# State-space loop prepared further ahead, swapped states from transposes, and the third block's tables loaded behind the last weights

## The chip, the cores and the metric

One core of a Trainium2 chip runs the whole program. TensorE (PE) does matmuls and transposes, VectorE (DVE) and ScalarE (ACT) the elementwise work, GpSimd (POOL) some of it, and SyncE (SP) issues the DMAs. The metric is the device time of one execution in microseconds (us), as the median of several; less is better.

## The reference

The program is a trunk of two layers over x (512 tokens, 1024 channels, fp32). The first mixes with attention, the second with a diagonal state-space model and a GLU; behind each stands an MLP with a squared ReLU.

```python
def reference(x, ...):
    for layer in range(DEPTH):
        h = rms_norm(x, mix_norm_g[layer])
        ...
            x = x + attn_mixer(h, ...)
        ...
            x = x + s5_mixer(h, ...)
        x = x + sq_relu_mlp(rms_norm(x, ffn_norm_g[layer]), w_ff1[layer], w_ff2[layer])

def s5_mixer(h, ...):
    ...
    def step(state, uc):
        bu = jnp.einsum('gpi,lbgi->lbgp', b_bar, uc.astype(jnp.complex64))
        _, hs = lax.associative_scan(combine, (a_el, bu), axis=0)
        hs = hs + a_pow[:, None] * state[None]
        y = jnp.einsum('gop,lbgp->lbgo', cmat, hs).real
        return hs[-1], y
    ...
    y = ys.transpose(2, 0, 1, 3, 4).reshape(B, S, D) + d_skip.astype(f32) * u
    g = jax.nn.gelu(y).astype(h.dtype)
    val, gate = jnp.split(g @ w_glu, 2, axis=-1)
    return val * jax.nn.sigmoid(gate)
```

There are 64 groups of 16 channels with 64 complex states each. A channel block below is 8 groups, that is 128 channels, so there are eight blocks.

## The kernel before

Every large product is made three times, from operands split into a high and a low fp32r part (`mm3`, L116 to L120). Weights come as 1 MB tiles `wraw` (DMA, L109), are cast to `whi` by ACT (L112), and DVE subtracts to get `wlo` (L113); the pool has two of each. The tile framework's scheduler sets the order of instructions on each engine, from the program's order and its own timeline. `behind(engine)` pins an instruction behind the newest one of an engine, `keep_in_program_order` fixes the row of DVE and POOL operations in the loop.

The stages are attention (to about 310 us), the first MLP (to 695.8), the state-space loop, the GLU's rest and the second MLP (from about 790 to the end). The first MLP has four groups of FF1 and FF2 products; an FF2 product has two column halves c = 0 and 1. Beside it a generator, `s5_tables` (L738 to L987), makes the loop's tables and puts them into DRAM; `pump` advances it by one step for each 6 us of planned matmul work. For each half block u its function `response` copies B into `bzh` and `bzl` (L946, L947) and at once multiplies with them on PE (L952 to L954). `B` itself is made by DVE (L888) and used by POOL products (L899 to L901).

Each block kb has four tables: tB, tT and tC of 1 MB and tR of 0.5 MB. `s5_open` (L1003) is called within the last FF2 product, behind the weights of c = 0, and loads the tables of kb 0 and 1 into a pool of two and those of kb 2 in pieces of 256 KB into the places of the MLP's input, `xhi` and `xlo`. The weights of c = 1 come behind that on SP. Later tables follow in the loop as places come free; tB and tC of kb 3 go into `wraw` tiles.

The loop in `s5` (L1121) runs ten iterations over eight blocks, with these steps:

- `s5_scale` (L1205): the block's input `ux` times the row norms on DVE, and the cast to Uh on ACT; `s5_split` (L1214): Ul on DVE.
- `s5_vee` (L1219): 24 matmuls U x tB, the copy `ys` on ACT (L1233), 8 transposes (L1237) that give V, real parts on partitions 0 to 63 and imaginary parts on 64 to 127.
- `s5_turn` (L1239): V times the rotation tR, one full product (L1246) and two of 64 partitions that read the other half of V (L1247, L1248); `s5_sub` (L1250) joins them.
- `s5_scan` (L1254): the scan over 64 chunks on DVE (L1260), behind the copy `dec` on ACT, then two products on POOL (L1261, L1262) that turn the states back; `s5_back2` (L1264) does the third on DVE, `s5_add` (L1269) joins them and casts Hh.
- `s5_out` (L1274): Hl on DVE, 48 matmuls U x tT and H x tC, two copies (L1293), 8 transposes (L1297); `s5_gelu` (L1299) makes the GLU's operands.

In iteration it the turn is that of block it, the scale, split and vee those of it + 1, the back2, add and out those of it - 1, the gelu that of it - 2. From it = 5 on `pieces` puts GLU products of the first output tile between; their weights are loaded and split at it = 4 (L1158).

Of the kernel before, what the change touches and what calls it, by code (L numbers as in the profile page):

```python
# [45 lines left out]
class Trunk:  # L46
# [690 lines left out]
    def s5_tables(self, s5p, s5b, s5c, s5d, gmix, side="right"):  # L737
# [6 lines left out]
        with ExitStack() as ctx:  # L744
# [196 lines left out]

            def response(u, wC):

                at = [bass.AP(tensor=t.tensor, offset=t.offset, ap=[t.ap[0], [64 + 16, 4], [1, 16]]) for t in bz]
                Bk = B[0][:, 4 * u:4 * u + 4]
                sc.copy(at[0], Bk)  # L946
                ve.tensor_sub(at[1], Bk, f32(at[0]))  # L947
                with tc.issue_after(self.last):
                    pk = self.ptp.tile([P, P], F32, name="pt")[:64]
                    for g4 in range(4):  # L950
                        wh, wl = (wC[:, a, g4, 16:144] for a in range(2))
                        pe.matmul(pk, bz[0][:, g4], wh, start=g4 == 0, stop=False)  # L952
# [21 lines left out]
            for u in range(16):  # L974
                now, made = made, make(u + 1) if u < 15 else None
                rotations(u // 2, u % 2)
                yield
                if wC is not None:
                    response(u - 1, wC)
                wC = split(u, *now)  # L980
                if u > 1:
                    expand(u - 2)
                yield
            response(15, wC)
            expand(14)
# [16 lines left out]

    def s5_open(self, places):  # L1003

        self.s5r, self.places, self.n_places = ExitStack(), places, 0
        self.tp = self.s5r.enter_context(self.tc.tile_pool(name="s5_t", bufs=2, side="right"))
        self.s5acc = self.tp.tile([P, S], F32, name="sacc", bufs=1)
        self.tabs = {}
        for kb in range(3):
            for n in ("tB", "tR", "tT", "tC"):  # L1010
                self.s5_load(kb, n, self.s5_pieces if kb == 2 else self.s5_whole)
        self.ux = []
# [68 lines left out]
    def s5(self, xT, w_glu, mlp, places):  # L1081
        nc, tc = self.nc, self.tc
        pe, ve, sc, gp = nc.tensor, nc.vector, nc.scalar, nc.gpsimd
        with ExitStack() as ctx:
            ctx.enter_context(places)
            sp = ctx.enter_context(tc.tile_pool(name="s5", bufs=2))
            sq = sp.tile([P, S], F32, name="gw")
            last = sc.activation(sq, xT[:, KT - 1], AF.Square).ins
# [9 lines left out]
            self.rsqrt(Rs, ps[:, :64], 1.0 / D, EPS, sp)  # L1098
            self.yv = sp.tile([P, 1024], F32, name="ys", bufs=1)
            dec = sp.tile([P, 8, 64], F32, name="dec", bufs=1)  # L1100
            gp.memset(dec[:, :, 0:1], 0.0)
            H = [[sp.tile([P, 8, 64], F32R, name=f"H{a}{b}", bufs=1) for a in "hl"] for b in range(2)]
            for a in range(2):
                for h in H[a]:
                    gp.tensor_scalar(h[:, :, 0:1], self.ones[:, 0:8][:, :, None], 0.0, None, op0=OP.mult)
            gT, st = [], {}
            pieces = {5: (0, 1), 6: (2, 3), 7: (4, 5), 8: (6,), 9: (7,)}
            half = [slice(0, 4), slice(4, 8)]
# [3 lines left out]
            for gs in half:  # L1112
                self.s5_split(0, st, gs)
                self.s5_vee(0, st, gs)

            def load(kb, n):
# [4 lines left out]
            for it in range(KT + 2):  # L1121
                if it < KT:
                    self.s5_turn(it, st, sp)
                if 0 < it <= KT:
                    self.s5_back2(it - 1, st)
                    if it != 3:
                        load(it + 2 if it < 3 else it + 1, "tR")
                if it + 1 < KT:
                    self.s5_scale(it + 1, st, Rs, sp, whole)
                if 0 < it <= KT:  # L1130
                    self.s5_add(it - 1, st, H[(it - 1) % 2])
                if it < KT:
                    self.s5_sub(it, st)
                if it + 1 < KT:
                    self.s5_split(it + 1, st, whole)
                    self.s5_vee(it + 1, st, whole)
                    if it == 0:
                        load(5, "tB")
                    elif 2 < it < 5:
                        load(it + 3, "tB")  # L1140
                    if 3 < it + 4 < KT:
                        with self.behind(nc.sync):
                            self.s5_load_x(it + 4)
                if it < KT:
                    self.s5_scan(it, st, dec)
                if 0 < it <= KT:
                    self.s5_out(it - 1, st, H[(it - 1) % 2], sp)
                    if it != 3:
                        load(it + 2 if it < 3 else it + 1, "tT")
                    if it < 3:  # L1150
                        load(it + 3, "tC")
                    elif it > 4:
                        load(it + 1, "tC")
                if it > 1:
                    gT.append([self.s5_place() for _ in "hl"])
                    self.s5_gelu(it - 2, st, gT[-1], sp)
                if it == 4:
                    W = self.glu_w(w_glu, 0)  # L1158
                    g = [self.glu(xT, W, gT, sp, 0, 0, [self.psp.tile([P, S], F32, name="s") for _ in range(2)])]
                for k in pieces.get(it, ()):  # L1160
                    g[0](k)
# [17 lines left out]
    def glu_w(self, w_glu, mp, eng=None):  # L1179

        return [self.load_wg([w_glu[kh * 512:(kh + 1) * 512, mp * 256:(mp + 1) * 256],
                              w_glu[kh * 512:(kh + 1) * 512, D + mp * 256:D + (mp + 1) * 256]], 4, eng)
                for kh in range(2)]

    def glu(self, xT, W, gT, sp, m, j, pss):
# [4 lines left out]
        def step(k):  # L1190
            if k is not None:
# [5 lines left out]
                return  # L1197
            th = sp.tile([P, S], F32, name="gw")
            sc.activation(th, pss[1], AF.Tanh, scale=0.5)
# [5 lines left out]
    def s5_scale(self, kb, st, Rs, sp, gs):  # L1205
        d = st.setdefault(kb, {})
        if "U" not in d:
            d["U"] = [sp.tile([P, 8, 64], F32R, name=f"U{a}", bufs=3) for a in "hl"]
        u = self.ux[kb][:, gs]
# [9 lines left out]
    def s5_vee(self, kb, st, gs):  # L1219
# [6 lines left out]
        for h in range(gs.start // 4, gs.stop // 4):  # L1226
            pc = self.mmp.tile([P, 4, P], F32, name="mm")
            for g4 in range(4):
# [3 lines left out]
                pe.matmul(pc[:64, g4], U[1][:, g8], tB(0, g8), start=False, stop=True)  # L1232
            sc.copy(vc[:, 4 * h:4 * h + 4], pc[:64])  # L1233
        if d["V"] is None:
            d["V"] = self.mmp.tile([P, 8, 64], F32, name="mm")
        for g8 in range(gs.start, gs.stop):
            pe.transpose(d["V"][:, g8], vc[:, g8], self.ident[64:, 64:])  # L1237

    def s5_turn(self, kb, st, sp):  # L1239
# [5 lines left out]
        R, V = d["R"], d["V"]  # L1245
        keep(ve.tensor_mul(d["t1"], V, R[0]))  # L1246
        keep(ve.tensor_mul(d["t2"][:64], V[64:], R[1][64:]))  # L1247
        keep(ve.tensor_mul(d["t2"][64:], V[:64], R[1][:64]))  # L1248

    def s5_sub(self, kb, st):  # L1250
        d = st[kb]
        self.tc.keep_in_program_order(self.nc.vector.tensor_sub(d["t1"], d["t1"], d["t2"]))

# [20 lines left out]
    def s5_out(self, kb, st, H, sp):  # L1274
# [5 lines left out]
        tT, tC = self.tabs[kb, "tT"], self.tabs[kb, "tC"]  # L1280
        ys = self.yv[:64].rearrange("p (l g o) -> p l g o", l=8, g=8)
        for h in range(2):
# [16 lines left out]
    def s5_gelu(self, kb, st, g, sp):  # L1299

        ve, sc = self.nc.vector, self.nc.scalar
        yT = st.pop(kb)["y"].rearrange("p l c -> p (l c)")
        w = sp.tile([P, S], F32, name="gw")
        sc.activation(w, yT, AF.Gelu_apprx_tanh)
# [4 lines left out]
class Mlp:  # L1309
# [41 lines left out]
    def run(self, emit=None, during=None, every=0.0, before_last=None, keep=False, halves=False):  # L1351
# [7 lines left out]
        with self.ctx if not keep else ExitStack(), tc.tile_pool(name="ffn_a", bufs=1) as pool:  # L1359
# [10 lines left out]
            for g in range(groups):  # L1370
# [30 lines left out]
                for c in range(2):  # L1401
                    W = [T.load_w(self.w2[g * GF * P + kh * 512:g * GF * P + (kh + 1) * 512,
                                          c * 512:(c + 1) * 512]) for kh in range(2)]
                    if last and c == 0 and before_last is not None:
                        with T.behind(nc.sync):
                            before_last()
                    for d4 in range(4):
# [29 lines left out]
def trunk(nc, tc, i, out):  # L1437
    with ExitStack() as ctx:
# [11 lines left out]
                              lambda xT: Mlp(T, xT, gf[0], i["w_ff1"][0], i["w_ff2"][0], "left"))  # L1450
        mlp.run(emit=lambda d, s: T.s5_emit(xT, d), before_last=lambda pool=mlp.pool: T.s5_open(pool), keep=True,
                during=T.s5_tables(i["s5p"], i["s5b"], i["s5c"], i["s5d"], i["mix_norm_g"][1]), every=6.0)
# [50 lines left out]
```

## Time and profile before

| what | us |
|---|---|
| median of 3 runs (1234.62 to 1238.17) | 1237.62 |
| the profiled execution | 1243.23 |
| its span, from the first instruction to the last | 1241.5 |
| PE busy in it | 1162.7 (94%) |
| DVE, ACT, POOL busy | 790.9, 495.0, 260.8 |
| first to last turn of the loop | 708.6 to 790.8 |

The trace is of the profiled execution. A number in brackets behind a row is idle time of the engine just before it, with what ended it. The granted clock (PEclk) is a share of 2.4 GHz: 1.00 is that level, 0.50 the lower one of 1.2 GHz, and numbers between are a mix. The DMA share is the mean busy share of the core's 16 DMA engines; it can come out slightly above 1.

### The profile page before, as it was taken

What the parts mean: (1) busy time and instruction counts of PE and PEld (TensorE: products, weight loads), DVE (VectorE), ACT (ScalarE), POOL (GpSimd) and SP (SyncE); (2) the same over time, 40 slices, a digit from 0 to 9 for tenths busy, and PEclk for the clock granted to TensorE, in tenths of its full rate; (3) what the DMA queues carried; (4) which work ended last, traced back from release to release, by engine and by line L of the source; (5) the groups of instructions that cost most, each with busy time, mean ns of one, the idle gap of its engine ahead of it and who ended that gap; (6) DMA issues with size and microseconds to landing.
All of it is one profiled execution on the core that took longest, in us unless ns stands there. A gap on an engine that the chain in (4) does not pass through costs nothing. (4 is left out here: it accounts for less than half of the span.)

```text
span 1241.5 us, 16297 instructions
## 1 busy us (share of the span) xinstructions
PE 1162.7 (94%) x6232; PEld 965.8 (78%) x6232; DVE 790.9 (64%) x1389; ACT 495.0 (40%) x919; POOL 260.8 (21%) x261
## 2 busy tenths in 40 slices
PE   7999999999999888999997668999999999999998
PEld 6878987778888666878886557778888888888887
DVE  8887765758889987779553567534444354444444
ACT  5857774544513333342342145443332241331321
POOL 5461031214001987505100022201000000000000
PEclk9999997999999889999998778999999999999999
DMA  6301201115423467874788577514223322322421
GB/s 219 103 1 52 69 35 35 35 35 191 121 79 102 163 197 228 245 222 142 245 288 299 160 230 252 214 34 133 79 94 102 102 86 84 102 102 68 132 86 54
DMA packets 123758, 161.94 MB, mean 130 GB/s; under 512 B 15648, under 2 KB 72352, under 8 KB 120992
## 3 DMA queue, kind: packets, MB, share of 16 engines
q1 hardware_dynamic: 123680, 160.90, 40.0%
q8 instruction: 49, 0.80, 0.3%
q14 instruction: 29, 0.24, 0.1%
HBM read 133.75 MB, written 35.52 MB: 136 GB/s over the span
## 5 line engine op out<-in xcount | busy, mean ns | idle before, releaser
L113 DVE TENSOR_TENSOR wlo<-wraw,whi 128x1024 fp32r<-128x1024 f32 x132 | 172.5, 1336 | 84.0 <-ACT whi L112 83.3
L112 ACT CAST whi<-wraw 128x1024 fp32r<-128x1024 f32 x132 | 131.9, 1049 | 228.4 <-PE mm L119 124.1
L118 PE MATMUL mm<-ahi,whi 128*128 128x512 f32 (+1 forms) x352 | 135.9, 388 | 7.7 <-ACT whi L112 7.7
L118 PE MATMUL mm<-xhi,whi 128*128 128x512 f32 x344 | 137.0, 398 | 0.0
L119 PE MATMUL mm<-xlo,whi 128*128 128x512 f32 x344 | 135.8, 395 | 0.0
L119 PE MATMUL mm<-alo,whi 128*128 128x512 f32 (+1 forms) x352 | 135.4, 387 | 0.0
L120 PE MATMUL mm<-xhi,wlo 128*128 128x512 f32 x344 | 134.4, 396 | 0.0
L120 PE MATMUL mm<-ahi,wlo 128*128 128x512 f32 (+1 forms) x352 | 134.2, 386 | 0.1
L118 PEld LDWEIGHTS mm<-ahi,whi 128*128 128x128 f32 x352 | 66.5, 189 | 21.1 <-ACT whi L112 8.1
L120 PEld LDWEIGHTS mm<-xhi,wlo 128*128 128x128 f32 x344 | 64.9, 189 | 15.6 <-DVE wlo L113 0.8
L120 PEld LDWEIGHTS mm<-ahi,wlo 128*128 128x128 f32 x352 | 66.3, 188 | 13.6 <-DVE wlo L113 0.5
L119 PEld LDWEIGHTS mm<-alo,whi 128*128 128x128 f32 x352 | 66.6, 189 | 13.1
L118 PEld LDWEIGHTS mm<-xhi,whi 128*128 128x128 f32 x344 | 64.9, 189 | 15.1 <-issue 0.5
L119 PEld LDWEIGHTS mm<-xlo,whi 128*128 128x128 f32 x344 | 65.0, 189 | 14.5 <-issue 0.2
L1418 DVE TENSOR_TENSOR mm<-mm,bcast 128x512 f32<-128x512 f32 (+1 forms) x44 | 29.8, 684 | 70.1 <-PE mm L120 70.1
L118 PE MATMUL s<-xhi,whi 128*128 128x512 f32 x168 | 66.7, 397 | 0.4 <-DVE fp L1390 0.4
L120 PE MATMUL s<-ahi,wlo 128*128 128x512 f32 x168 | 66.1, 394 | 0.9 <-DVE wlo L113 0.8
L119 PE MATMUL s<-xlo,whi 128*128 128x512 f32 x168 | 66.5, 396 | 0.0
L120 PE MATMUL s<-xhi,wlo 128*128 128x512 f32 x168 | 66.3, 396 | 0.0
L118 PE MATMUL s<-ahi,whi 128*128 128x512 f32 x168 | 66.2, 395 | 0.0
L119 PE MATMUL s<-alo,whi 128*128 128x512 f32 x168 | 66.0, 393 | 0.0
L899 POOL TENSOR_TENSOR W<-PW,B 128x512 f32<-128x512 f32 x16 | 23.8, 1490 | 160.1 <-DVE B L888 141.4
(487 smaller groups left out, 2868.0 us busy)
## 6 DMA issues: line engine op xcount, KB each, us to landing
wraw<-in_w_ff SPq DMA_DIRECT2D x64, 1024.0 KB
dC<-wC SPq DMA_DIRECT2D x16, 512.0 KB
dB<-wB SPq DMA_DIRECT2D x16, 512.0 KB
wraw<-in_w_glu SPq DMA_DIRECT2D x16, 512.0 KB
tT<-dT SPq DMA_DIRECT2D x7, 1024.0 KB
wraw<-in_w_in SPq DMA_DIRECT2D x24, 256.0 KB
tB<-dB SPq DMA_DIRECT2D x6, 1024.0 KB
tC<-dC SPq DMA_DIRECT2D x6, 1024.0 KB
```

Of the source, the lines that this page charges most:

```text
L112: nc.scalar.copy(hi[:, s, :n], raw[:, s, :n])
L113: nc.vector.tensor_sub(lo[:, s, :n], raw[:, s, :n], f32(hi)[:, s, :n])
L118: te.matmul(ps, whi, xhi, start=start, stop=False)
L119: te.matmul(ps, whi, xlo, start=False, stop=False)
L120: self.last = te.matmul(ps, wlo, xhi, start=False, stop=stop).ins
L899: gp.tensor_mul(dst, pw[a][:, :, 1:9, None].to_broadcast(bc), B[a][:, gs][:, :, None, :].to_broadcast(bc))
L1418: ve.tensor_mul(ps[:, s], ps[:, s], self.Rb[:, s])
```

## The change

The change has three parts.

*Tables of kb 2.* `s5_open` takes c: for c = 0 it loads the tables of kb 0 and 1, for c = 1 those of kb 2, behind the weights of c = 1.

*The generator.* `place(u)` makes `bzh` and `bzl` in the step ahead of the one in which `response(u)` uses them; there is one step more at the end.

*The loop.* Block 1 is scaled ahead of the loop and block it + 2 in iteration it. Split and vee of it + 1 come right behind the turn. The scan goes to the end of the iteration. V is made twice, as it was and with its halves swapped, by 16 transposes; ACT copies the real part once more behind the imaginary one for that (the tile `ys` grows to 1536 columns). The turn is then two full products and `s5_sub` an addition. There are four Uh in place of three, one Hl in place of two, one `gw` in place of two. The raw GLU weights are requested at it = 4 and split at it = 5 and 6, and fewer GLU products stand at it = 5.

```diff
-            def response(u, wC):
+            def place(u):
...
                 sc.copy(at[0], Bk)
                 ve.tensor_sub(at[1], Bk, f32(at[0]))
+
+            def response(u, wC):
...
                 rotations(u // 2, u % 2)
+                if u:
+                    place(u - 1)
                 yield
...
+            place(15)
+            yield
             response(15, wC)
...
-    def s5_open(self, places):
-
+    def s5_open(self, places, c):
+
+        if c:
+            for n in ("tB", "tR", "tT", "tC"):
+                self.s5_load(2, n, self.s5_pieces)
+            return
...
-        for kb in range(3):
+        for kb in range(2):
             for n in ("tB", "tR", "tT", "tC"):
-                self.s5_load(kb, n, self.s5_pieces if kb == 2 else self.s5_whole)
+                self.s5_load(kb, n, self.s5_whole)
...
-            pieces = {5: (0, 1), 6: (2, 3), 7: (4, 5), 8: (6,), 9: (7,)}
+            pieces = {5: (0,), 6: (1, 2), 7: (3, 4), 8: (5, 6), 9: (7,)}
...
+            self.s5_scale(1, st, Rs, sp, whole)
...
                 if it < KT:
                     self.s5_turn(it, st, sp)
-                if 0 < it <= KT:
-                    self.s5_back2(it - 1, st)
-                    if it != 3:
-                        load(it + 2 if it < 3 else it + 1, "tR")
-                if it + 1 < KT:
-                    self.s5_scale(it + 1, st, Rs, sp, whole)
-                if 0 < it <= KT:
-                    self.s5_add(it - 1, st, H[(it - 1) % 2])
-                if it < KT:
-                    self.s5_sub(it, st)
                 if it + 1 < KT:
                     self.s5_split(it + 1, st, whole)
                     self.s5_vee(it + 1, st, whole)
...
+                if 0 < it <= KT:
+                    self.s5_back2(it - 1, st)
+                    if it != 3:
+                        load(it + 2 if it < 3 else it + 1, "tR")
+                    self.s5_add(it - 1, st, H[(it - 1) % 2])
                 if it < KT:
-                    self.s5_scan(it, st, dec)
+                    self.s5_sub(it, st)
+                if it + 2 < KT:
+                    self.s5_scale(it + 2, st, Rs, sp, whole)
...
+                if it < KT:
+                    self.s5_scan(it, st, dec)
                 if it == 4:
-                    W = self.glu_w(w_glu, 0)
+                    with self.behind(nc.sync):
+                        raw = [self.glu_raw(w_glu, 0, kh) for kh in range(2)]
+                if it in (5, 6):
+                    W = [] if it == 5 else W
+                    W.append(self.split_w(raw[it - 5], 4, 512))
...
-            sc.copy(vc[:, 4 * h:4 * h + 4], pc[:64])
+            sc.copy(vc[:, 4 * h:4 * h + 4, :P], pc[:64])
+        sc.copy(vc[:, gs, P:], f32(vc[:, gs, :64]))
         if d["V"] is None:
-            d["V"] = self.mmp.tile([P, 8, 64], F32, name="mm")
-        for g8 in range(gs.start, gs.stop):
-            pe.transpose(d["V"][:, g8], vc[:, g8], self.ident[64:, 64:])
+            d["V"] = [self.mmp.tile([P, 8, 64], F32, name="mm") for _ in range(2)]
+        for a in range(2):
+            for g8 in range(gs.start, gs.stop):
+                pe.transpose(d["V"][a][:, g8], vc[:, g8, 64 * a:64 * a + P], self.ident[64:, 64:])
...
-        keep(ve.tensor_mul(d["t1"], V, R[0]))
-        keep(ve.tensor_mul(d["t2"][:64], V[64:], R[1][64:]))
-        keep(ve.tensor_mul(d["t2"][64:], V[:64], R[1][:64]))
+        keep(ve.tensor_mul(d["t1"], V[0], R[0]))
+        keep(ve.tensor_mul(d["t2"], V[1], R[1]))
...
-                    if last and c == 0 and before_last is not None:
+                    if last and before_last is not None:
                         with T.behind(nc.sync):
-                            before_last()
+                            before_last(c)
```

The queue of SP within the last FF2 product, in the kernel before; `wraw` are the weights, `xlo` and `xhi` the pieces of kb 2:

```order
L1046 DMA tR_6850<-dR1_125 128x512 x2
L1051 DMA tT_6853<-dT1_117 128x2048
L1051 DMA tC_6855<-dC1_93 128x2048
L1051 DMA xlo_6871<-dT2_118 128x512
L1051 DMA xhi_6872<-dT2_118 128x512
L1051 DMA xlo_6877<-dC2_94 128x512
L1051 DMA xhi_6878<-dC2_94 128x512
L1051 DMA xlo_6879<-dC2_94 128x512
L1051 DMA xhi_6880<-dC2_94 128x512
L109 DMA wraw_7013<-in_w_ff2 128x4x512
L109 DMA wraw_7021<-in_w_ff2 128x4x512
```

The weights of c = 1 are the last two rows. The same queue after the change, from the first half of these weights on:

```order
L109 DMA wraw_6985<-in_w_ff2 128x4x512
L965 DMA dK7h_114<-Ks_6728 4x16x128
L965 DMA dK7l_115<-Ks_6728 4x16x128
L971 DMA dT7_123<-dK7h_114 128x4x128
L971 DMA dT7_123<-dK7l_115 128x4x128
L1062 DMA tB_6839<-dB0_84 128x2048
L1057 DMA tR_6841<-dR0_124 128x512 x2
L1062 DMA tT_6844<-dT0_116 128x2048
L1062 DMA tC_6846<-dC0_92 128x2048
L1062 DMA tB_6848<-dB1_85 128x2048
L1057 DMA tR_6850<-dR1_125 128x512 x2
L1062 DMA tT_6853<-dT1_117 128x2048
```

Then the table of kb 1 that is left, the second half of the weights, and only then kb 2:

```order
L1062 DMA tC_6855<-dC1_93 128x2048
L109 DMA wraw_6993<-in_w_ff2 128x4x512
L1062 DMA xlo_7001<-dB2_86 128x512
L1062 DMA xhi_7002<-dB2_86 128x512
L1062 DMA xlo_7003<-dB2_86 128x512
L1062 DMA xhi_7004<-dB2_86 128x512
```

So both halves of the weights now stand ahead of kb 2. Next, DVE in one iteration of the loop, it = 2, before (t1 and t2 are the turn's results, `ux_7057` the input of block 3):

```order
L1246 TENSOR_TENSOR t1_7437<-mm_7356,xlo_6865 128x512
L1247 TENSOR_TENSOR t2_7438<-mm_7356,xhi_6866 64x512
L1248 TENSOR_TENSOR t2_7438<-mm_7356,xhi_6866 64x512
L1267 TENSOR_TENSOR u2_7312<-t2_7311,tR_6850 64x512
L1211 TENSOR_TENSOR ux_7057<-ux_7057,Rs_7179 128x512
L1271 TENSOR_TENSOR t1_7310<-t1_7310,u2_7312 128x512
L1252 TENSOR_TENSOR t1_7437<-t1_7437,t2_7438 128x512
L1306 TENSOR_TENSOR xhi_7565<-gw_7566,xlo_7564 128x512
L1217 TENSOR_TENSOR Ul_7448<-ux_7057,Uh_7447 128x512
L1260 SCALAR_TENSOR_TENSOR t2_7438<-dec_7196,t1_7437 128x512
L1279 TENSOR_TENSOR Hl1_7201<-t1_7310,Hh1_7200 128x8x63
```

And after, in the same iteration (`ux_7326` is the input of block 4):

```order
L1266 TENSOR_TENSOR t1_7468<-mm_7367,xlo_7009 128x512
L1267 TENSOR_TENSOR t2_7469<-mm_7368,xhi_7010 128x512
L1235 TENSOR_TENSOR Ul_7393<-ux_7057,Uh_7392 128x512
L1286 TENSOR_TENSOR u2_7334<-t2_7333,tR_6850 64x512
L1290 TENSOR_TENSOR t1_7332<-t1_7332,u2_7334 128x512
L1271 TENSOR_TENSOR t1_7468<-t1_7468,t2_7469 128x512
L1229 TENSOR_TENSOR ux_7326<-ux_7326,Rs_7179 128x512
L1298 TENSOR_TENSOR H2_7200<-t1_7332,H1_7199 128x8x63
L1325 TENSOR_TENSOR xhi_7601<-gw_7602,xlo_7600 128x512
L1279 SCALAR_TENSOR_TENSOR t2_7469<-dec_7196,t1_7468 128x512
```

Ul moved to the place behind the turn, the scale is that of a later block, Hl moved ahead of the scan. Last, PE around the second half of V's transposes for block 2, before (H are the operands of `s5_out` for block 0):

```order
L1292 MATMUL pt_7398<-tC_6846,Hl0_7199 64x128
L1237 MATMUL mm_7356<-ident_73,ys_7195 128x64 x4
L1287 MATMUL pt_7398<-tT_6844,Uh_7206 64x128
L1288 MATMUL pt_7398<-tT_6844,Uh_7206 64x128
L1289 MATMUL pt_7398<-tT_6844,Ul_7207 64x128
```

And around the transposes of the swapped V after the change:

```order
L1311 MATMUL pt_7425<-tC_6846,H2_7200 64x128
L1306 MATMUL pt_7425<-tT_6844,Uh_7204 64x128
L1307 MATMUL pt_7425<-tT_6844,Uh_7204 64x128
L1308 MATMUL pt_7425<-tT_6844,Ul_7205 64x128
L1257 MATMUL mm_7368<-ident_73,ys_7195 128x64 x8
L1309 MATMUL pt_7425<-tC_6846,H0_7198 64x128
```

The swapped V is a row of eight transposes of its own that stands among the matmuls of `s5_out`, behind those that read Hl (`H2`).

## Rows read from the trace of the kernel before

**Rows 1.** Page, part 1: busy time, share, instructions of each engine.

```profile
PE 1162.7 (94%) x6232; PEld 965.8 (78%) x6232; DVE 790.9 (64%) x1389; ACT 495.0 (40%) x919; POOL 260.8 (21%) x261
```

**Rows 2.** Waits, 655 to 680 us: total, times, longest.

```profile
PE mm L118 <- ACT whi L112: 7.7, 1, 7.7
...
ACT whi L112 <- DMA wraw<-in_w_ff: 10.4, 2, 9.9
```

**Rows 3.** Timeline of SP and PE, 649 to 673 us: start, length, instruction.

```profile
649.93 0.32 SPq L1051 DMA_DIRECT2D tC<-dC  x1
...
659.30 0.32 SPq L1051 DMA_DIRECT2D xhi<-dC  x1
661.80 2.87 SPq L109 DMA_DIRECT2D wraw<-in_w_ff  x2
...
672.19 0.80 PE L118 MATMUL mm<-ahi,whi 128*128 128x512 f32 x1 [7.70 <-ACT whi L112]
```

**Rows 4.** Windows of the last FF2: length, engines busy (instructions), clock, DMA share, GB/s.

```profile
645.00:665.00 20.00, 19.49 (x86) 15.79 (x85) 9.71 (x15) 3.99 (x8) 0.00 (x0) 1.00 1.02 404
...
672.20:676.00 3.80, 3.80 (x10) 3.04 (x11) 3.80 (x4) 3.37 (x4) 0.00 (x0) 0.58 0.34 132
```

**Rows 5.** Waits of PE, 300 to 664 us.

```profile
PE pt L952 <- ACT bzh L946: 7.5, 2, 4.4
PE pt L954 <- DVE bzl L947: 6.3, 3, 4.1
```

**Rows 6.** Line L1246, the turn: instructions, durations in ns, first and last start.

```profile
L1246 DVE TENSOR_TENSOR t<-mm,tR x7: 691/692/693, 708.6 to 790.8; 128x512 f32<-128x512 f32 x7
```

**Rows 7.** Windows from turn to turn (PE, PEld, DVE, ACT, POOL busy; clock; DMA).

```profile
708.60:716.70 8.10, 4.45 (x32) 3.71 (x32) 5.20 (x8) 2.39 (x4) 2.55 (x2) 0.50 0.42 134
716.70:727.90 11.20, 7.08 (x64) 6.56 (x65) 6.90 (x11) 3.57 (x6) 2.86 (x3) 0.56 0.65 178
727.90:738.80 10.90, 8.16 (x86) 7.13 (x86) 7.46 (x12) 6.46 (x10) 2.84 (x2) 0.84 0.80 273
738.80:754.40 15.60, 11.59 (x107) 9.86 (x108) 10.90 (x13) 8.09 (x14) 3.19 (x2) 0.78 0.89 297
754.40:768.40 14.00, 10.99 (x82) 8.91 (x83) 9.74 (x13) 5.28 (x9) 2.85 (x2) 0.76 0.75 242
768.40:779.70 11.30, 9.91 (x117) 8.31 (x117) 7.48 (x11) 5.70 (x11) 2.86 (x2) 1.00 0.67 238
779.70:790.80 11.10, 8.33 (x71) 6.99 (x72) 7.51 (x12) 4.52 (x8) 2.87 (x2) 0.85 0.63 238
```

**Rows 8.** Waits, 720 to 800 us.

```profile
DVE t L1246 <- PE mm L1237: 18.5, 5, 4.2
```

**Rows 9.** Chain that ended last, 768 to 782 us: start, length, what.

```profile
769.53 0.06 PE pt L1287
...
771.22 8.36 DMA tR<-dR
```

**Rows 10.** Timeline of one period, DVE, POOL and PE.

```profile
727.87 0.69 DVE L1246 TENSOR_TENSOR t<-mm,xlo 128x512 f32<-128x512 f32 x1 [4.25 <-PE mm L1237]
...
733.61 1.22 DVE L1260 TENSOR_TENSOR_SCAN t<-dec,t 128x512 f32<-128x512 f32 x1
...
734.97 1.57 POOL L1261 TENSOR_TENSOR u<-t,xhi 64x512 f32<-64x512 f32 x1 [8.86 <-DVE t L1260]
736.62 1.27 POOL L1262 TENSOR_TENSOR t<-t,xlo 128x512 f32<-128x512 f32 x1
...
737.40 0.46 PE L1237 MATMUL mm<-ident,ys 64*128 64x64 f32 x4
```

**Rows 11.** Window 400 to 420 us, columns as in rows 4.

```profile
400.00:420.00 20.00, 16.08 (x75) 12.65 (x73) 20.00 (x16) 9.06 (x15) 19.92 (x16) 0.98 0.34 118
```

**Rows 12.** Timeline of PE: eight transposes of V in two periods.

```profile
715.29 1.36 PE L1237 MATMUL mm<-ident,ys 64*128 64x64 f32 x8
...
767.66 0.71 PE L1237 MATMUL mm<-ident,ys 64*128 64x64 f32 x8
```

More of the change, by code (lines that the diff above doesn't have):

```diff
@@ L1086, in s5 @@
             sp = ctx.enter_context(tc.tile_pool(name="s5", bufs=2))
-            sq = sp.tile([P, S], F32, name="gw")
+            sq = sp.tile([P, S], F32, name="gw", bufs=1)
             last = sc.activation(sq, xT[:, KT - 1], AF.Square).ins
@@ L1098, in s5 @@
             self.rsqrt(Rs, ps[:, :64], 1.0 / D, EPS, sp)
-            self.yv = sp.tile([P, 1024], F32, name="ys", bufs=1)
+            self.yv = sp.tile([P, 1536], F32, name="ys", bufs=1)
             dec = sp.tile([P, 8, 64], F32, name="dec", bufs=1)
             gp.memset(dec[:, :, 0:1], 0.0)
[L1102 to L1105, printed above, removed]
+            H = [sp.tile([P, 8, 64], F32R, name=f"H{a}", bufs=1) for a in range(3)]
+            for h in H:
+                gp.tensor_scalar(h[:, :, 0:1], self.ones[:, 0:8][:, :, None], 0.0, None, op0=OP.mult)
+            H = [(H[a], H[2]) for a in range(2)]
             gT, st = [], {}
-            pieces = {5: (0, 1), 6: (2, 3), 7: (4, 5), 8: (6,), 9: (7,)}
+            pieces = {5: (0,), 6: (1, 2), 7: (3, 4), 8: (5, 6), 9: (7,)}
             half = [slice(0, 4), slice(4, 8)]
@@ L1140, in s5 @@
                         load(it + 3, "tB")
-                    if 3 < it + 4 < KT:
-                        with self.behind(nc.sync):
-                            self.s5_load_x(it + 4)
-                if it < KT:
-                    self.s5_scan(it, st, dec)
+                if 0 < it <= KT:
[3 more added lines that the diff above has]
+                    self.s5_add(it - 1, st, H[(it - 1) % 2])
+                if it < KT:
+                    self.s5_sub(it, st)
+                if it + 2 < KT:
+                    self.s5_scale(it + 2, st, Rs, sp, whole)
+                if 3 < it + 4 < KT:
+                    with self.behind(nc.sync):
+                        self.s5_load_x(it + 4)
                 if 0 < it <= KT:
@@ L1156, in s5 @@
                     self.s5_gelu(it - 2, st, gT[-1], sp)
+                if it < KT:
+                    self.s5_scan(it, st, dec)
                 if it == 4:
-                    W = self.glu_w(w_glu, 0)
+                    with self.behind(nc.sync):
+                        raw = [self.glu_raw(w_glu, 0, kh) for kh in range(2)]
+                if it in (5, 6):
+                    W = [] if it == 5 else W
+                    W.append(self.split_w(raw[it - 5], 4, 512))
+                if it == 5:
                     g = [self.glu(xT, W, gT, sp, 0, 0, [self.psp.tile([P, S], F32, name="s") for _ in range(2)])]
@@ L1179, in glu_w, with glu_raw @@
     def glu_w(self, w_glu, mp, eng=None):
-        return [self.load_wg([w_glu[kh * 512:(kh + 1) * 512, mp * 256:(mp + 1) * 256],
-                              w_glu[kh * 512:(kh + 1) * 512, D + mp * 256:D + (mp + 1) * 256]], 4, eng)
-                for kh in range(2)]
+        return [self.split_w(self.glu_raw(w_glu, mp, kh), 4, 512, eng) for kh in range(2)]
+    def glu_raw(self, w_glu, mp, kh):
+        return self.raw_w([w_glu[kh * 512:(kh + 1) * 512, mp * 256:(mp + 1) * 256],
+                           w_glu[kh * 512:(kh + 1) * 512, D + mp * 256:D + (mp + 1) * 256]], 4)
     def glu(self, xT, W, gT, sp, m, j, pss):
@@ L1197, in step @@
                 return
-            th = sp.tile([P, S], F32, name="gw")
+            th = sp.tile([P, S], F32, name="gw", bufs=1)
             sc.activation(th, pss[1], AF.Tanh, scale=0.5)
@@ L1207, in s5_scale @@
         if "U" not in d:
-            d["U"] = [sp.tile([P, 8, 64], F32R, name=f"U{a}", bufs=3) for a in "hl"]
+            d["U"] = [sp.tile([P, 8, 64], F32R, name="Uh", bufs=4), sp.tile([P, 8, 64], F32R, name="Ul", bufs=3)]
         u = self.ux[kb][:, gs]
@@ L1245, in s5_turn @@
         R, V = d["R"], d["V"]
[L1246 to L1248 removed]
+        keep(ve.tensor_mul(d["t1"], V[0], R[0]))
+        keep(ve.tensor_mul(d["t2"], V[1], R[1]))
     def s5_sub(self, kb, st):
         d = st[kb]
[L1252 removed]
+        self.tc.keep_in_program_order(self.nc.vector.tensor_add(d["t1"], d["t1"], d["t2"]))
     def s5_scan(self, kb, st, dec):
@@ L1280, in s5_out @@
         tT, tC = self.tabs[kb, "tT"], self.tabs[kb, "tC"]
-        ys = self.yv[:64].rearrange("p (l g o) -> p l g o", l=8, g=8)
+        ys = self.yv[:64, :1024].rearrange("p (l g o) -> p l g o", l=8, g=8)
         for h in range(2):
@@ L1302, in s5_gelu @@
         yT = st.pop(kb)["y"].rearrange("p l c -> p (l c)")
-        w = sp.tile([P, S], F32, name="gw")
+        w = sp.tile([P, S], F32, name="gw", bufs=1)
         sc.activation(w, yT, AF.Gelu_apprx_tanh)
@@ L1450, in trunk @@
                               lambda xT: Mlp(T, xT, gf[0], i["w_ff1"][0], i["w_ff2"][0], "left"))
-        mlp.run(emit=lambda d, s: T.s5_emit(xT, d), before_last=lambda pool=mlp.pool: T.s5_open(pool), keep=True,
+        mlp.run(emit=lambda d, s: T.s5_emit(xT, d), before_last=lambda c, pool=mlp.pool: T.s5_open(pool, c), keep=True,
                 during=T.s5_tables(i["s5p"], i["s5b"], i["s5c"], i["s5d"], i["mix_norm_g"][1]), every=6.0)
```

## The prediction

> **What bounds the kernel now.** I read the page's busy shares first, then the waits and windows of the stretches in which TensorE is not full. TensorE is the bound: 1162.7 of 1241.5 us [rows 1], and the second MLP behind the state-space loop is packed. So only places where PE stands still, or runs at the lower of its two clocks (1.2 instead of 2.4 GHz), are worth anything, and this change touches three of them.
>
> First, the last FF2 product of the first MLP. PE waits 7.7 us there, once, for a weight cast on ACT, and ACT waited 9.9 us for the weight DMA [rows 2]. SP's rows tell why: the tables of block kb 2 were issued up to 659.30, the two weight DMAs only at 661.80, and PE starts again at 672.19 [rows 3]. The DMA engines were full meanwhile, share 1.02 at 404 GB/s from 645 to 665, and behind the wait PE is at clock 0.58: 10 matmuls in 3.80 us where 86 took 19.49 us before [rows 4]. At 0.227 us each that is 3.80 - 2.27 = 1.5 us more. The place costs 9.2 us.
>
> Second, the table generator beside the first MLP. PE's `response` matmuls wait 7.5 us for `bzh` (ACT, L946) and 6.3 us for `bzl` (DVE, L947), 13.8 us together [rows 5].
>
> Third, the loop. `s5_turn` begins for kb 0 at 708.6 and for kb 7 at 790.8 [rows 6], 82.2 us for seven periods of 8.1, 11.2, 10.9, 15.6, 14.0, 11.3 and 11.1 us, the windows that I cut there; PE is busy 60.5 us of them and its clock is 0.50 to 1.00 [rows 7]. The wait that ends last is the turn's on the transposes of V: 18.5 us of the waits between 720 and 800 [rows 8]. Once it is a table: the chain has a tR that took 8.36 us to land, ahead of the turn of kb 6 [rows 9]. One period reads: turn at 727.87, scan at 733.61 (1.22 us), POOL from 734.97, the transposes from 737.40, the next turn behind them [rows 10]. U of the next block is scaled only after the turn, so cast, 24 matmuls, copy and transposes stand one behind the other in each period.
>
> **The change part by part.**
>
> *Kb 2's tables behind the weights: -9.2 us.* SP now issues the first half of the c = 1 weights ahead of all tables and the second behind kb 0 and 1; kb 2's fourteen transfers follow. Ahead of the second half stand 7 MB (two blocks of 3.5); at 404 GB/s [rows 4] that is 17.3 us. Kb 1's last table left SP at 649.93 [rows 3]; the queue is shorter now by six pieces of kb 2, so I place the weights at 660 to 666, where PE needs them some 7 us after the first half, from about 671 on. I take the whole 9.2; a late second half would leave 3 to 4 us, so 6 is the lower end. Behind them, kb 2's 3.5 MB needs 8.7 us and is wanted in the loop's second iteration; the share of 0.34 from 672.2 to 676.0 [rows 4] leaves room.
>
> *`place` one generator step earlier: -4 us.* It moves two small operations per tile and adds nothing but a step. Gain at most 13.8. But DVE is busy 20.00 and POOL 19.92 of the 20 us from 400 to 420 [rows 11]: what made `bzl` late is a full DVE queue, and an operation put in earlier still waits for the `B` that those two make. Some of the waits move on to the next tile. Between 0 and 13.8 I take 4, nearer to the lower end because the queue that made the operand late stays as full.
>
> *The loop: -14.2 us.* Scaling two blocks ahead and splitting right behind the turn takes ux, cast and Ul off the path. What remains per period: DVE does two turns (0.69 each, one 64-partition operation fewer), Ul, back2, add, sub, ux, Hl, gelu and the scan, 9 x 0.65 + 1.22 = 7.1 us. In the order, the swapped V's transposes stand behind some 20 of `s5_out`'s matmuls, which need Hl, the eighth DVE operation. Hl ends 8 x 0.65 = 5.2 us behind the turn's start (POOL's 1.57 + 1.27 us [rows 10] lie under the turn, Ul and back2), and the swapped V is wanted 0.65 us behind the next turn's start, so 4.6 us count; then come 44 matmuls and 8 transposes: at full clock 44 x 0.06 + 0.71 = 3.4 us, at half clock 44 x 0.129 + 1.36 = 7.0 us [rows 9, 12] (0.129 is what 24 matmuls of the first period took: 4.45 us busy for 32 instructions, 8 of them transposes of 1.36 together [rows 7, 12]). The added PE work is 8 transposes, the added ACT work one copy of half a tile; both lie inside that. The period is 8.0 us warm and 11.6 cold. PE has 72 matmuls and 24 transposes per period, 72 x 0.06 + 24 x 0.09 = 6.5 us, 80% of 8.0, against 4.45 of 8.1 to 9.91 of 11.3 us now [rows 7]; I expect the clock to be down in the first two periods, of which it 0 has no `s5_out` yet, and up later. So it 0 to 3: 8.5 + 10.5 + 9 + 8 = 36 us in place of 45.8.
>
> Then the DMA engines bind. In the seven windows their busy time is 3.4 + 7.3 + 8.7 + 13.9 + 10.5 + 7.6 + 7.0 = 58.4 us [rows 7], and nothing of it is removed; in the order the raw GLU weights stand ahead of tR of kb 6 and 7. At the best share that the loop shows, 0.89, this needs 65.6 us, at 0.80 it needs 73. I take 68, that is 32 for it 4 to 6 in place of 36.4 (in it 6 DVE and ACT also split GLU weights). Ends: 58 (a share of 1.0, as beside the MLP) and 80 (hardly a change).
>
> *What it adds: +2 us.* Ahead of kb 0's turn stand 8 more transposes (1.36 us at the half clock [rows 12]) and two short copies, while one product is spread over both halves: +1. Behind the loop six GLU matmuls, moved past the last turn, against an earlier last `s5_out`: 0 to 2, I take 1.
>
> Sum: 1243.2 - 9.2 - 4 - 14.2 + 2 = 1217.8 us for the profiled execution. It was 5.6 above the median of 1237.6, so **1212 us**.
>
> The Trainium skill (TensorE: Matmul & The Clock Gate, Part 4: PE-mode transpose) says that transposes don't count as busy for the clock as matmuls do. The rows here show transposes at either clock, 8 in 1.36 and in 0.71 us [rows 12], behind matmuls that were at the same clock. By the page the doubled transposes would win no clock, which speaks for rival C.
>
> The skill's page SBUF: State Buffer (section SBUF: two separate sides) says that a VectorE operation with two SBUF inputs and a GpSimd operation lock each other out for their whole length. The row from 400 to 420, both engines full, agrees [rows 11]. By it Ul and back2 would stretch beside POOL, about 1 us a period, and the loop would be 75 us, which is a part of the way to rival A.
>
> **The rivals.**
> *A, the loads bind the loop.* tR of kb 5 to 7 and the tables land late, and the turn waits for DMA in place of transposes. For it: the 8.36 us landing [rows 9] and the share of 0.75 to 0.89 in the slowest windows; against it: shares of 0.42 and 0.65 in the first two leave room [rows 7]. Loop 80: 1237.6 - 9.2 - 4 - 2 + 2 = 1224.
> *B, everything is hidden.* Loop at a DMA share of 1.0, 58 us, and `place` worth 8: 1237.6 - 9.2 - 8 - 24 + 2 = 1198. For it: 1.02 beside the MLP; against it: that was one run of large transfers.
> *C, slower: the clock stays down.* The first period ran at clock 0.50 throughout [rows 7]. At that rate 72 x 0.129 + 24 x 0.17 = 13.4 us, seven times 94 us, without the GLU's: +11.6. With nothing from `place`: 1237.6 + 11.6 + 2 - 9.2 = 1242. It decides from a loop of over 90 us. Against it: 768.4 to 779.7 ran at 1.00 with 9.91 of 11.3 us busy [rows 7].
> *D, the change doesn't do what it says.* The second half of the weights comes too late behind 7 MB (5 us of wait stay), `place` gives 0, the loop gains 7: 1237.6 - 4 - 7 + 2 = 1229.
>
> **How the numbers follow.** Forecast (1203 to 1219) 0.54; A 0.21; B 0.11; D 0.08; C 0.06. The range leaves out the outer half of B, half of D and C, and takes in the sizes of `place` and the loop: 1198 to 1228. A measurement of this kernel tells about 0.3% from no change, 1233.9 to 1241.3. Faster: forecast, A, B and most of D, 0.91. C stands at that border, so it is shared: same 0.04 with what is left of D, slower 0.05.
>
> **What would show it.** In the profile after: no wait of PE on `whi` L112 near 665, and the weights issued on SP ahead of kb 2; waits on `bzh` and `bzl` down to some 10 us from 13.8, with DVE still full near 410; the first turn to the last 68 us, with the clock above 0.8 from the third period; the turn waiting on transposes early and on tR late. The forecast is wrong if the loop's clock stays at 0.5 to 0.6, if DVE's operations beside POOL stretch far above 0.69 us, if the wait on `whi` reappears at the second half, or if the stretch behind the last turn, 450.7 us now, grows by more than 2.

## The result

The changed kernel takes 1220.19 us in the median of 4 runs (1214.39 to 1222.52), the kernel before 1237.89; the ratio is 0.9848, with an interval of 0.9802 to 0.9895. In a second comparison with more runs (e1, below) it is 1216.56 against 1240.56, ratio 0.9804 (0.9775 to 0.9832). That is some 18 and 24 us less. The profiled execution of after took 1218.8 us, span 1217.1, 24.4 less than that of before.

The page of after, part 1, then the clock in 40 slices:

```profile
PE 1159.6 (95%) x6296; PEld 966.4 (79%) x6296; DVE 782.8 (64%) x1381; ACT 500.6 (41%) x928; POOL 259.6 (21%) x260
...
PEclk9999997999999998999999778999999999999999
```

PE's busy time fell by 3.1 us only (1162.7 in [rows 1]); most of what went is idle time. To see where, I cut both traces at the same instructions of DVE: the first `fp` of the first MLP, the first and the last `xT` of its last FF2 product (L1390 and L1419, in after L1409 and L1438). Timeline of before:

```profile
310.68 0.69 DVE L1390 SCALAR_TENSOR_TENSOR fp<-mm,fr 128x512 f32<-128x512 f32 x1 [3.21 <-ACT fr L1389]
...
656.44 0.68 DVE L1419 TENSOR_TENSOR xT<-xT,mm 128x512 f32<-128x512 f32 x1
...
696.50 0.69 DVE L1419 TENSOR_TENSOR xT<-xT,s 128x512 f32<-128x512 f32 x1
```

and of after:

```profile
309.61 0.69 DVE L1409 SCALAR_TENSOR_TENSOR fp<-mm,fr 128x512 f32<-128x512 f32 x1 [3.21 <-ACT fr L1408]
...
650.32 0.68 DVE L1438 TENSOR_TENSOR xT<-xT,mm 128x512 f32<-128x512 f32 x1
...
680.90 0.69 DVE L1438 TENSOR_TENSOR xT<-xT,s 128x512 f32<-128x512 f32 x1
```

The turn's line in after, with its first and last start (the one of before is [rows 6]):

```profile
L1266 DVE TENSOR_TENSOR t<-mm,tR x7: 665/692/693, 693.6 to 765.1; 128x512 f32<-128x512 f32 x7
```

| stretch | before | after | change | predicted |
|---|---|---|---|---|
| attention, to the first `fp` | 310.7 | 309.6 | -1.1 | 0 |
| first MLP with the generator | 345.8 | 340.7 | -5.1 | -4 |
| last FF2 product | 40.1 | 30.6 | -9.5 | -9.2 |
| to the first turn | 12.1 | 12.7 | +0.6 | +1 |
| first to last turn | 82.2 | 71.4 | -10.7 | -14.2 |
| behind the last turn | 450.7 | 452.0 | +1.3 | +1 |
| profiled execution | 1243.2 | 1218.8 | -24.4 | -25.4 |

In the last FF2 product PE is busy without a gap from 650 to 670 us and at the full clock, while DMA is as full as before (SP's timeline and the windows of after; [rows 3, 4] are those of before). The `wraw` row is the second half of the weights:

```profile
644.18 0.32 SPq L1062 DMA_DIRECT2D tC<-dC  x1
644.89 0.38 SPq L109 DMA_DIRECT2D wraw<-in_w_ff  x1
...
664.84 0.32 SPq L1062 DMA_DIRECT2D xlo<-dC  x1
```

```profile
650.00:660.00 10.00, 10.00 (x45) 8.27 (x45) 7.74 (x11) 3.76 (x5) 0.00 (x0) 1.00 1.02 403
660.00:670.00 10.00, 10.00 (x46) 8.27 (x45) 3.89 (x5) 2.49 (x3) 0.00 (x0) 1.00 0.99 365
```

PE's waits beside the generator, 310 to 655 us in after: `bzh` is gone, `bzl` stays with 7.9, and a wait on POOL's W is new. These three come to 11.5 us in place of 13.8.

```profile
PE pt L957 <- DVE bzl L947: 4.7, 3, 2.3
PE pt L920 <- POOL W L901: 3.6, 1, 3.6
PE pt L955 <- DVE bzl L947: 3.2, 1, 3.2
```

The whole stretch, and the part of it from 400 to 500 us, show where its 5 us went (before, then after; columns as in [rows 7]):

```profile
310.70:656.40 345.70, 329.12 (x1572) 269.36 (x1571) 278.31 (x488) 122.71 (x215) 123.79 (x96) 0.97 0.59 188
400.00:500.00 100.00, 85.69 (x400) 68.04 (x399) 87.13 (x101) 37.37 (x75) 82.08 (x71) 0.90 0.59 189
```

```profile
309.60:650.30 340.70, 325.27 (x1572) 267.20 (x1571) 275.98 (x488) 122.31 (x215) 124.41 (x96) 0.98 0.59 186
400.00:500.00 100.00, 84.57 (x412) 67.03 (x411) 88.96 (x105) 36.85 (x75) 82.48 (x70) 0.95 0.62 197
```

PE's idle time in the stretch fell from 16.6 to 15.4 us only. The other 3.9 us are busy time: the same 1572 instructions took 325.3 us in place of 329.1, at a higher granted clock.

The windows from turn to turn in after (columns as in [rows 7]):

```profile
693.60:700.40 6.80, 4.81 (x35) 3.98 (x36) 4.32 (x6) 3.00 (x5) 1.90 (x2) 0.50 0.72 283
700.40:707.20 6.80, 6.04 (x46) 5.26 (x47) 6.27 (x9) 2.85 (x5) 0.65 (x1) 0.50 0.76 237
707.20:719.40 12.20, 10.83 (x115) 9.75 (x115) 7.09 (x12) 7.21 (x12) 2.56 (x2) 0.78 0.69 233
719.40:728.50 9.10, 8.12 (x93) 6.92 (x91) 6.84 (x11) 6.51 (x11) 3.08 (x3) 0.91 0.88 308
728.50:741.60 13.10, 11.07 (x148) 9.87 (x148) 7.69 (x12) 8.06 (x14) 4.89 (x4) 0.99 0.77 263
741.60:752.50 10.90, 8.80 (x77) 8.02 (x78) 8.73 (x12) 6.95 (x10) 2.87 (x2) 0.54 0.78 265
752.50:765.10 12.60, 12.60 (x124) 10.77 (x123) 8.70 (x13) 6.41 (x11) 1.70 (x2) 1.00 0.89 306
```

It 0 to 3 take 34.9 us (36 predicted), it 4 to 6 take 36.6 (32 predicted, 36.4 before). DVE's timeline shows what stands ahead of the late turns:

```profile
736.24 1.22 DVE L1279 TENSOR_TENSOR_SCAN t<-dec,t 128x512 f32<-128x512 f32 x1
740.98 0.69 DVE L1325 TENSOR_TENSOR xhi<-gw,xlo 128x512 fp32r<-128x512 f32 x1 [3.52 <-ACT xlo L1324]
741.59 0.68 DVE L1266 TENSOR_TENSOR t<-mm,tR 128x512 f32<-128x512 f32 x1
...
749.93 2.68 DVE L172 TENSOR_TENSOR wlo<-wraw,whi 128x1024 fp32r<-128x1024 f32 x2 [2.04 <-ACT whi L171]
752.54 0.68 DVE L1266 TENSOR_TENSOR t<-mm,tR 128x512 f32<-128x512 f32 x1
```

No turn waits for tR there. Ahead of the turn of kb 5 stands a gelu operation that waits 3.52 us for ACT, ahead of that of kb 6 two subtractions of GLU weights that wait 2.04. In it 6 PE is full: the GLU products fill it. A turn behind such a row would also hide a table that lands while DVE waits, so this trace alone doesn't tell when tR came. All that the loop gained lies in it 0 to 3, 34.9 us in place of 45.8.

### The profile page after: what moved, and what is told of

It reads as the page before. It is cut to its first block, busy times and chain, and to the rows that moved or that the text cites. A ratio compares the mean times of both kernels' runs of the same rounds, so it can differ in the third digit from the quotient of the medians.

```text
span 1217.1 us, 16430 instructions
## 1 busy us (share of the span) xinstructions
PE 1159.6 (95%) x6296; PEld 966.4 (79%) x6296; DVE 782.8 (64%) x1381; ACT 500.6 (41%) x928; POOL 259.6 (21%) x260
## 5 line engine op out<-in xcount | busy, mean ns | idle before, releaser
L113 DVE TENSOR_TENSOR wlo<-wraw,whi 128x1024 fp32r<-128x1024 f32 x132 | 169.7, 1315 | 81.1 <-ACT whi L112 80.9
L118 PEld LDWEIGHTS mm<-xhi,whi 128*128 128x128 f32 x344 | 64.7, 188 | 16.6 <-ACT whi L112 1.8
L119 PEld LDWEIGHTS mm<-alo,whi 128*128 128x128 f32 x352 | 66.2, 188 | 13.1
L120 PEld LDWEIGHTS mm<-xhi,wlo 128*128 128x128 f32 x344 | 64.5, 188 | 14.8 <-issue 0.2
L899 POOL TENSOR_TENSOR W<-PW,B 128x512 f32<-128x512 f32 x16 | 26.4, 1650 | 155.5 <-DVE B L888 141.5
```

What stands on the lines that cost most here:

```text
L113: nc.vector.tensor_sub(lo[:, s, :n], raw[:, s, :n], f32(hi)[:, s, :n])
L118: te.matmul(ps, whi, xhi, start=start, stop=False)
L119: te.matmul(ps, whi, xlo, start=False, stop=False)
L120: self.last = te.matmul(ps, wlo, xhi, start=False, stop=stop).ins
L899: gp.tensor_mul(dst, pw[a][:, :, 1:9, None].to_broadcast(bc), B[a][:, gs][:, :, None, :].to_broadcast(bc))
```

## The experiments

Two theories of the 3.5 us by which the loop missed its forecast: D, the step of the prediction, that the loads bind it 4 to 6; O, that DVE's order does. The loop below is first to last turn of each profile.

**e1, the changed kernel again**, no edit.

> The changed kernel once more, as the control for the three runs beside it, since the medians differ by 17.7 us and the two profiled executions by 24.4. Theory (the traces give the size: 9.5 from the tables, 5.1 from the generator, 10.7 from the loop, -1.3 behind it, 1 from the attention stage by chance): 21 to 25 us less than the kernel before. Rival (the profiled execution of before was a late one): 16 to 19 us less.

1216.56 us, 24.0 less than before: as the theory says. Its loop is 72.1 us.

**e2, kb 2's tables back**, with the second half of the weights behind them:

```diff
         if c:
-            for n in ("tB", "tR", "tT", "tC"):
-                self.s5_load(2, n, self.s5_pieces)
             return
```

> The changed kernel with kb 2's tables loaded with those of kb 0 and 1 again, ahead of the second half of the last weights. Theory: PE waits for whi of the second half again, 8 to 10 us more than the control. Rival (the first half of the weights, which now stands ahead of all tables, hides most of it, or the DMA engines were full anyway): 0 to 4 us more.

1220.48 us, 3.9 more than the control, and the theory falls: PE has no wait on `whi`, and the last FF2 product takes 31.1 us (651.22 to 682.27), 0.5 more than the control's. The first half of the weights stands ahead of all tables here, as in after, and PE works off what needs it first. The two profiled executions differ by 5.1 us, of which the rest lies in attention (1.7), the loop (0.9) and the stretch behind it (2.0). The 3.9 us aren't clear of noise: the first series of the unedited kernel had a median of 1220.19.

**e9, the tables alone**, the same part put into the kernel before.

> The kernel before with nothing changed but that kb 2's tables are loaded behind the c = 1 weights. Theory: PE's wait of 7.7 us and the half clock behind it go, c = 1's first product is 9 to 10 us shorter, the whole 8 to 11 us less than before; the loop stays at 80 to 84 us. Rival (from e2, where undoing this part cost 3.9 us): 3 to 5 us less, since both halves still stand behind 7 MB of tables.

1230.08 us, 9.1 less (ratio 0.9926, 0.9902 to 0.9951). Both halves of the weights stand behind the tables of kb 0 and 1 and ahead of kb 2's, and the last FF2 product takes 30.7 us (656.18 to 686.83) in place of 40.1. So the stall needed both halves behind all three blocks of tables; it goes when either one half goes ahead (e2) or kb 2 goes behind (e9). The first half is ahead in the kernels with the new generator step (after, e2, e4) and behind the tables of kb 0 and 1 in those without it (e3, e9): in the change two parts each remove the stall, and e2 took back only one of them. The loop, unchanged, takes 79.2 us in place of 82.2, a little below the 80 to 84 expected.

SP's timeline of e9, kb 1's last table and both halves behind it:

```profile
645.44 0.32 SPq L1055 DMA_DIRECT2D tC<-dC  x1
646.14 4.74 SPq L109 DMA_DIRECT2D wraw<-in_w_ff  x2
```

**e3, `place` back** into `response`:

```diff
-                if u:
-                    place(u - 1)
                 yield
...
             def response(u, wC):
+                place(u)
```

> The changed kernel with place inside response again. Theory: the stretch of the first MLP with the generator is 5 us longer (the difference of the traces), so 4 to 6 us more than the control, with waits on bzh back. Rival (the order of a full DVE decides, not the step): within 2 us of the control.

1226.26 us, 9.7 more than the control. The waits of before are back (310 to 660 us):

```profile
PE pt L958 <- DVE bzl L947: 6.7, 4, 4.1
PE pt L956 <- ACT bzh L946: 6.5, 2, 3.9
```

The stretch with the generator takes 346.4 us in place of 340.6, 5.8 more, as the theory says; the 9.7 of the whole are more than its 4 to 6. Most of the remaining difference of the profiles lies in the attention stage (3.9 us), which the edit doesn't touch. What the step changes is again PE's busy time, not its idle time. In the three profiles without it (before, e3, e9) the stretch takes 343.9 to 346.4 us with PE busy 329.1 to 330.5 and idle 14.8 to 16.6; in the eleven with it, 340.3 to 342.0 us with PE busy 323.5 to 326.4 and idle 14.0 to 17.2.

**e4, the loop back**: the kernel before with the two other parts.

> The kernel before with place and kb 2's tables changed, its loop left as it was. Theory: first to last turn 80 to 84 us in place of 71.4, so 9 to 12 us more than the control. Rival (the loop was slow only because kb 2's tables and the stall ahead of it left the clock down and the DMA queues late): first to last turn under 76 us, 0 to 5 us more.

1224.93 us, 8.4 more than the control; the loop takes 78.7 us. Both lie between theory and rival, nearer the theory. So of the 10.7 us that the loop lost, some 3 came with the tables' part (82.2 to 79.2 in e9, 78.7 here; one profile each) and about 7 (78.7 to 71.4 in after, 72.1 in e1) with the loop's own edits.

**e5, no table loads in the loop** for kb 4 to 7:

```diff
-                if kb < KT:
+                if 3 < kb < KT:
+                    self.tabs[kb, n] = self.tabs[1, n]
+                elif kb < KT:
```

> The loop without the table loads of kb 4 to 7, whose iterations use the tables of kb 1 instead (a part of the computation is left out); with the loads gone, the scheduler also puts the GLU weights' splits an iteration earlier. Theory D (the step of the prediction: the DMA engines bind it 4 to 6): first to last turn falls from 72 to 58 to 64 us. Theory O (DVE's order binds them: an operation that waits for ACT stands ahead of a turn whose operands are there, and later the GLU matmuls fill PE): 68 to 73 us, with the same waits.

The loop takes 64.8 us (the whole 1213.99): below what O says, just above what D says. It 4 to 6 take 28.0 us in place of 36.6, and it 3, into which the first of the splits moved, 11.1 in place of 9.1. So without the loads these iterations are far shorter, and O alone can't be all of it; but the edit moves the splits too, so it doesn't part the two theories.

**e6, gelu behind Hl:**

```diff
-        ve.tensor_sub(g[1], w, f32(g[0]))
+        with self.behind(ve):
+            ve.tensor_sub(g[1], w, f32(g[0]))
```

> gelu's DVE operation of each block held behind the Hl of its iteration, so that it no longer stands ahead of the next turn. Theory O: DVE's wait of 3.5 us ahead of the turn of block 5 goes, period it 4 falls from 13.1 to about 10.5 us, the loop to about 69. Theory D: the turn then waits for tR or tB, and the period stays within 1 us of 13.1.

It 4 falls from 13.1 to 10.5 us, as O says. But then the turn of kb 5 waits for tR, the weights' subtraction longer for a late weight, and the DMA engines are full (DVE's timeline, then the windows of it 5 and 6):

```profile
742.98 0.69 DVE L1266 TENSOR_TENSOR t<-mm,tR 128x512 f32<-128x512 f32 x1 [2.21 <-DMA tR<-dR]
...
752.64 2.45 DVE L172 TENSOR_TENSOR wlo<-wraw,whi 128x1024 fp32r<-128x1024 f32 x2 [2.53 <-ACT whi L171]
```

```profile
743.00:755.20 12.20, 10.84 (x95) 9.65 (x95) 9.36 (x13) 8.46 (x13) 3.09 (x3) 0.72 0.93 309
755.20:765.70 10.50, 10.32 (x81) 8.28 (x80) 8.54 (x11) 5.08 (x9) 0.17 (x1) 1.00 1.01 373
```

The loop is 68.2 us, beside the 68 that I predicted with the loads as its bound: it 4 to 6 take 33.2, of which it 5 became longer (12.2 for 10.9) and it 6 shorter (10.5 for 12.5). The whole, 1215.83, can't be told from the control.

**e7, the weights' low parts on POOL** as well, `split_w(raw[it - 5], 4, 512, gp)`.

> As e6, and the low parts of the first GLU weights are made by POOL in place of DVE, so that neither stands ahead of a turn. Theory O: it 5 loses the wait of 2.0 and the 2.6 us of two subtractions ahead of the turn of block 6, so 10.9 becomes about 8 to 9, and the loop is 64 to 67 us, the whole 4 to 6 us less than the control. Rival (POOL, at about 2.6 us for each of four halves and locked against DVE, delays the scan's products and PE's GLU matmuls): the loop is 70 us or more and the whole no better.

The rival holds: 1220.98 us, loop 72.6, it 6 takes 15.1. POOL needs 10.30 us for the four halves, and beside it DVE's operations on two SBUF tiles stretch from 0.69 to as much as 2.75 us, and its turns wait 7.3 us for tR. Of these, 5.28 us stand ahead of the turn of kb 6: with the gelu and the weights' subtractions both gone from DVE's queue, it 5 still takes 12.2 us, and what it waits for is a load.

```profile
752.61 10.30 POOL L172 TENSOR_TENSOR wlo<-wraw,whi 128x1024 fp32r<-128x1024 f32 x4
...
755.05 0.69 DVE L1266 TENSOR_TENSOR t<-mm,tR 128x512 f32<-128x512 f32 x1 [5.28 <-DMA tR<-dR]
756.28 1.65 DVE L1235 TENSOR_TENSOR Ul<-ux,Uh 128x512 fp32r<-128x512 f32 x1
757.96 2.75 DVE L1286 TENSOR_TENSOR u<-t,tR 64x512 f32<-64x512 f32 x1
760.81 2.65 DVE L1290 TENSOR_TENSOR t<-t,u 128x512 f32<-128x512 f32 x1
```

**e8, V once**, turned in three products as before.

> The changed loop with V transposed once and the turn in three products again; the order ahead of that is as in the change. Theory (what the loop gained came from preparing a block further ahead): the loop is 71 to 75 us, within 3 of the control. Rival (the swapped V matters, by one DVE operation a period and full partitions): 77 us or more.

1218.59 us, loop 70.9, behind it 450.3. The loop's gain comes with the rest of its edits, the new order above all; the second set of transposes isn't shown to buy anything.

**e10, e6 with the second raw GLU weights an iteration later:**

```diff
-                if it == 4:
+                if it in (4, 5):
...
-                if it in (5, 6):
+                if it in (5, 7):
```

> As e6, with the second half of the first GLU weights requested an iteration later, behind tR, tT and tC of kb 6, and split at it = 7. Theory (after e6 the loads bind it 5 and 6): the waits of the turns on tR go, it 5 and it 6 fall from 22.7 to 19 to 21 us, the loop to 65 to 67. Rival (DVE's wait on the first half's cast binds it 5 and PE it 6): 22 us or more, the loop 68 or more.

1216.16 us. It 5 and 6 take 11.8 + 12.0 = 23.8 us: the rival. That the loop is 67.2 all the same comes from it 2, 10.5 us in place of 12.2, with the same instructions there in the same order. The windows of it 2 in e1 and in e10 differ in the clock:

```profile
706.40:718.50 12.10, 10.73 (x115) 9.65 (x115) 6.99 (x11) 7.14 (x12) 2.56 (x2) 0.78 0.87 282
```

```profile
704.50:715.00 10.50, 9.15 (x126) 8.17 (x125) 7.01 (x11) 7.72 (x13) 2.58 (x2) 1.00 0.75 253
```

**e11, the gelu table early**, one tiny gelu ahead of the loop.

> As e10, with one tiny gelu on ACT ahead of the loop, so that its table load of 1.28 us no longer stands ahead of the cast of H in it = 2. Theory: period it 2 falls from 12.2 to 10 to 11 us, the loop by as much. Rival (PE's half clock sets it 2, not ACT's queue): 11.8 us or more.

It 2 takes 10.8 us. That is what the theory asks for, and yet it doesn't show it: e10 had 10.5 with the table load still in its place. The loop takes 68.6 us, and the stretch from the last FF2 product to the first turn grew from 12.7 to 14.2 us. 1217.61 us.

**e12, e11 with V once.**

> As e11, with V transposed once and the turn in three products. Theory from e8 (the second set of transposes buys nothing): the loop within 2 us of e11's, the stretch behind it 1 us shorter, the whole equal or 1 to 2 us less. Rival (with the waits gone, the DVE operation more per period shows): the loop 3 us or more longer than e11's.

1217.66 us, loop 70.2 against 68.6, behind it 448.3 against 450.2: no difference in the whole, for the second time. None of e6, e7, e8, e10, e11 and e12 beats the changed kernel beyond its interval.

## Why the prediction was right, and where it was off

**The stall** (-9.2, measured -9.5, and -9.1 when the part is made alone): right in place, size and mechanism. That the first half of the weights ahead would have been enough (e2), and that the generator's step puts it there, I hadn't seen.

**`place`** (-4, measured -5.1, and 5.8 back in e3): right in size, but not for the reason given, and so by luck. I took 4 us of PE's waits. DVE and POOL stayed full and part of the waits moved on, to W, as I said, but so much of them that PE's idle time fell by 1.2 us only, and over the 14 profiles it doesn't depend on the step at all. What the step gave is 3.9 us of PE's busy time, at a granted clock of 0.95 in place of 0.90 from 400 to 500 us. Why the clock stood higher, no run shows.

**The loop** (-14.2, measured -10.7): the step that failed is "then the DMA engines bind", 32 us for it 4 to 6, which took 36.6. The sum of DMA time was right (56 us in after, at a mean share of 0.79, beside the 0.80 that I gave 73 us for), but DMA wasn't what came last in all three. In it 4 DVE's order stood ahead of it, with 2.6 us that e6 gives back; only with that removed is the turn late for tR. In it 6 PE was full of GLU products, which the sum didn't have. In it 5 the loads are the bound that I took: it takes 12.2 us with a late tR even when nothing stands ahead of its end (e7). Besides, about 3 us of the 10.7 belong to the tables' part (e9, e4).

It 0 to 3 came out at 34.9 for 36, by luck, from errors that cancel: it 0 and 1 took 6.8 each in place of 8.5 and 10.5, though at the half clock all along, and it 2 12.2 in place of 9, with its clock at 0.78. I had put 44 matmuls of `s5_out` into it 1; in the trace nearly all of them stand in it 2.

**What it adds** (+2, measured +1.9 with 0.6 ahead of the loop and 1.3 behind): right, as far as 2 us can be told: the stretch behind the loop took 451.3 us in e1 and 453.3 in e3, with the same code in it.

**The sum for the profile** was 1217.8 and the profile took 1218.8. That it is so near is luck as well: the loop gave 3.5 us less, and attention, which the change doesn't touch, and the generator each 1.1 more. The median missed by 8 us, 1212 for 1220.19: I carried over that the profiled execution of before was 5.6 above its median. That of after was 1.4 below. With the larger series of e1 the median is 1216.56, 4.6 off.

**The rivals.** A (loads) holds in it 5, and elsewhere only behind DVE's order. B fell: the loop is 71. C fell: the clock was 0.50 for two periods, as expected, then 0.54 to 1.00; but it was 0.78 in it 2 and 0.54 in it 5, where I had named 0.8 from the third period on as a sign. D fell. The transposes' rule of the Trainium skill (TensorE: Matmul & The Clock Gate, Part 4: PE-mode transpose) can't be told here: the first three periods ran at 0.50, 0.50 and 0.78 with 16 transposes of V, and at 0.50, 0.50 and 0.79 with 8 (e8). The lock of the Trainium skill's page SBUF: State Buffer (section SBUF: two separate sides) shows in e7's rows, 0.69 to 2.75 us, but costs DVE nothing in after: there POOL runs mostly while DVE waits, and Ul and back2 kept 0.69 us.

## What to carry to other kernels

Cut both traces at the same instructions and compare stretch by stretch; a total mixes a change of 10 us with up to 6 us that an untouched stage moves by itself. Split each stretch into the bound engine's idle and busy time before you name the cause: the generator's step was meant to save waits, and what it saved was busy time at the lower clock. Where an engine works in order, look at what stands ahead of the late instruction in its queue before you blame the resource that it needs: an operation off the path that waits for a third engine can cost as much as a late load, and the load shows only when it is gone. A transfer that stalls the bound engine can be cured at either end, by moving the needed one ahead or the bulky one behind; one half of the weights ahead was enough.

## What was not expected of the hardware

The attention stage, the same code in all 14 profiles, ends (first `fp`) between 307.2 us (e10) and 313.1 us (e5); that alone is half a per cent of the whole. The same instructions of it 2 took 12.1 or 10.5 us as the granted clock was 0.78 or 1.00; six more profiles with that order took 12.0 to 12.5 us at 0.77 or 0.78. What sets the one or the other from run to run stays open.
